# One rounding operation of 2048 columns per unit and engine, with five fixed slots for its parts

## The chip, the cores and the metric

The kernel runs on one core of a Trainium2 chip. Its time is the device time of one execution in microseconds (us), the median over several runs. A core has a matrix engine (PE, whose weight loads are shown as PEld), VectorE (DVE), ScalarE (ACT), GpSimd (POOL) and SyncE (SP, which issues most transfers here). Each engine takes its instructions strictly in order and waits on semaphores for what other engines or transfers deliver.

## The reference, cut to what matters

One decoder layer over 256 tokens of width 2048: latent attention with 16 heads and a short gated convolution side by side, each with a gate, merged by sigmoid gates, then one output projection.

```python
h = _rmsnorm(x, pre_norm_g)
proj = jnp.einsum('bsd,de->bse', h, w_in)          # then cut into ten parts
q = jnp.einsum('bsr,re->bse', _rmsnorm(q_a, q_a_norm_g), w_q_b)
kv = jnp.einsum('bsr,re->bse', _rmsnorm(c_kv, kv_a_norm_g), w_kv_b)
...
attn = attn.reshape(b, s, MLA_WIDTH) * jax.nn.silu(z_mla)
y_mla = jnp.einsum('bse,ed->bsd', attn, w_o_mla)
...
y_conv = jnp.einsum('bse,ed->bsd', b_gate * conv * jax.nn.silu(z_conv), w_o_conv)
merged = jax.nn.sigmoid(g_mla) * y_mla + jax.nn.sigmoid(g_conv) * y_conv
out = jnp.einsum('bsd,de->bse', merged, w_out)
x = x + _rmsnorm(out, post_norm_g)
```

All of it is float32. The kernel makes float32 products on PE out of three products of rounded parts: each operand is split into a high part (the value rounded) and a low part (what the rounding left), and hi x hi, hi x lo and lo x hi are added.

## The kernel before, in words

**Units.** The weights come in units of 128 partitions by 2048 columns (1 MB, `UNIT`, L38), loaded by SP into three rotating buffers `raw`. Before PE can use a unit it is rounded: `split_act` (L264 to L271) writes the high part with one ScalarE operation (L265, `whi`) and the low part with one VectorE subtraction (L266, `wlo`). It does so by halves of 1024 columns (`HALF`), so a unit takes two operations on each engine. The halves lie in two pools of five rotating tiles each, tags `whi` and `wlo`. A half's buffer comes free when PE has done its last product from the half five places earlier.

**PE's work on a unit.** A plain unit is 24 products of 512 columns: first 16 with high weights (against the high and the low part of the activations), then 8 with low weights. Through the first 16 it alternates: four products with the first half, four with the second, and again; then two and two of the 8. A paired unit is 12 products: 8 and 4.

**The stages.** From the start to about 75 us come the latent projections and the gates of the first heads. Then 16 heads follow, each with its own weights (`group_a`, `group_r`, `values`, `channels`) and its softmax, to about 595 us. Behind the heads stands one list, `seq`, of units. It holds plain blocks of four units (their accumulators are named `sq`, the units 115 to 118 being the first block, over the attention output `at_both`), and between them four sets of paired units (`s0` to `s3`, accumulators `sX`, `sY`, `sZ`), which form products of sums of weights: names Q1, V5, V6, V7, V3, V4, Q2, two units each. Where the operand of a paired unit is a sum, VectorE adds two units first (L1272, 2048 columns). V5's operand of the first set is `first_rt` after `first_rb` was added, V6's is the same tile after `first_rc` was added too. Units 113 and 114 are Q1 of the first set and are rounded from `first_rt0` and `first_rt1`. At the end comes the out projection.

**What sets the order.** `ahead` loads up to three units and rounds one unit ahead of the one taken. Behind the heads the loop at L1440 walks over `seq`: for position j it first issues the rounding of the units up to j + 2, then the products of j. Within one engine the order of the program isn't kept as written: a scheduler moves instructions by its own estimate of times, except those marked with `keep_in_program_order` (the last two arguments of `split_act` decide that for a rounding). So a change of what is issued moves instructions on ACT and DVE, and their order is then fixed for every execution.

**The last head.** In the last head (h = 15) `split_branch(3)` rounds the last quarter of the attention output `at_f` into `at_both3`. Ahead of it unit 115 is loaded and rounded (L1101).

Of the kernel before, what the change touches and what calls it, by code (L numbers as in the profile page):

```python
# [12 lines left out]
F32R = mybir.dt.float32r  # L13
# [5 lines left out]
P = 128  # L19
# [63 lines left out]
def tile_layer(ctx: ExitStack, tc: tile.TileContext, xw, w0, xb, x, pos, pvec, post_g, wc, wz, wcv, wkr, wqk, wqr, wv, cwr, wsq, out):  # L83
# [64 lines left out]

    raws, splits, early = {}, {}, {}
# [26 lines left out]
    def split_unit(i):  # L176
        t, w = raws.pop(i), plan[i][1]
        parts = []
        if i == u_kr:
            t = t[:, :w].rearrange("p (k c) -> p k c", k=KD)  # L180
            for h in range(2):
                both = wpool.tile([P, HALF], F32R, name=f"whi{i}_{h}", tag="whi", bufs=5)
                both = both[:, :].rearrange("p (k j c) -> p k j c", k=KD // 2, j=2)
# [5 lines left out]
        if i <= u_qa[-1]:  # L189

            hi, lo = (wpool.tile([P, HALF], F32R, name=f"{o}{i}", tag=o, bufs=5) for o in ("whi", "wlo"))
# [6 lines left out]
            return  # L198
        for h in range(0, w, HALF):
            n = min(HALF, w - h)  # L200
            if u_out[3, 0] <= i < u_out[3, 3]:
                both = spool.tile([P, 2, HALF], F32R, name=f"whl{i}_{h}", tag=LAST[len(last_parts)], bufs=1)
                last_parts.append(both)
                hi, lo = both[:, 0, :], both[:, 1, :]
            else:
                hi = wpool.tile([P, HALF], F32R, name=f"whi{i}_{h}", tag="whi", bufs=5)
                lo = wpool.tile([P, HALF], F32R, name=f"wlo{i}_{h}", tag="wlo", bufs=5)
            split_act(hi[:, :n], lo[:, :n], t[:, h : h + n], i in (u_head[0][1], *u_first, *u_d[0][2][:2]), i in (u_grp["r", 0], u_grp["v", 0], u_head[0][0]))
            parts.append((hi, lo))
# [407 lines left out]
    def group_a(g, together=False):  # L617
# [8 lines left out]
        if g == 0:  # L626

            fs = list(fs)
            ahead(u_grp["v", 0])
# [364 lines left out]
    for h in range(H):  # L994
# [105 lines left out]
        if h == H - 1:  # L1100
            load_raw(done["raw"])  # L1101
            split_unit(done["split"])
            done.update(raw=done["raw"] + 1, split=done["split"] + 1)
# [22 lines left out]
    last_parts = []  # L1126
# [123 lines left out]
    def paired(i, n, c, combine):  # L1250
# [14 lines left out]
        def split(name, u, src, plus, then):  # L1265
            def go():
# [6 lines left out]
                out = []  # L1273
                for h in range(2):
                    hi = wpool.tile([P, HALF], F32R, name=f"shi{i}_{name}{u}_{h}", tag="whi", bufs=5)
                    lo = wpool.tile([P, HALF], F32R, name=f"slo{i}_{name}{u}_{h}", tag="wlo", bufs=5)
                    split_act(hi[:, :], lo[:, :], t[:, h * HALF : (h + 1) * HALF])
                    out.append((hi, lo))
                if then:
                    add_by_transfer(raw[then[0], u], then[1], 2 + u)  # L1280
                return pieces(out)
# [156 lines left out]
    ns = 0  # L1438
    ready = {}
    for j in range(-1, len(seq)):  # L1440
        while loads and loads[0][1] <= j:
            loads.pop(0)[2]()
        if j < 0:
            continue
# [224 lines left out]
```

## Time and profile before

| | us |
|---|---|
| median of 3 runs | 1013.83 (1013.68 to 1014.23) |
| the profiled execution | 1013.55 |
| its span | 1011.8 |
| PE busy | 1004.2 (99%) |
| DVE busy | 811.4 (80%) |
| ACT busy | 586.3 (58%) |
| POOL busy | 170.7 (17%) |

The granted clock of PE was 0.998 of full speed. A profile row of a group reads: line, engine, operation, out<-in with sizes, count, busy time and mean ns of one, then the engine's idle time just before them and what ended it. A row of the timeline begins with the start in us and a duration, and ends with how many instructions in a row it stands for; the last result of the row can lie a little behind the next start, since an engine begins the next operation before the last one's end. In a row of PE's waits stands who waited, for whom, and for how long in total, how often and the longest.

### The profile page before, as it was taken

How to read it: one execution, taken by the hardware profiler on the slowest of the kernel's cores; microseconds unless marked ns; L12 is line 12 of the kernel's file. 1: busy time of each engine (PE TensorE's matmuls, PEld its weight loads, DVE VectorE, ACT ScalarE, POOL GpSimd, SP SyncE). 2: the span in 40 equal slices, each digit the busy share in tenths (PEclk: the TensorE clock that was granted, in tenths of full speed). 3: DMA queues.
4: the chain of work that ended last, by engine and by line, in shares of the span. 5: the costliest groups of instructions: out<-in, count | busy, mean ns of one | idle time of the engine just before them, and what ended most of it. 6: DMA issues, size and time to landing. Idle time of an engine off the chain costs nothing.

```text
span 1011.8 us, 12983 instructions
## 1 busy us (share of the span) xinstructions
PE 1004.2 (99%) x4552; PEld 835.4 (83%) x4552; DVE 811.4 (80%) x1111; ACT 586.3 (58%) x838; POOL 170.7 (17%) x311
## 2 busy tenths in 40 slices
PE   9999999999999999999999999999999999999997
PEld 7888888888888888888888888888888888888886
DVE  7588878868888689877797889898989779997562
ACT  7675656556556456555565465565675664674541
POOL 4620411113211223212133110000000001003000
PEclk9999999999999999999999999999999999999999
DMA  8785768568786668866689779897599989639742
GB/s 338 282 291 183 260 201 304 197 214 276 234 303 232 228 229 283 272 219 232 216 264 338 292 306 291 344 375 218 187 333 296 305 321 260 239 127 322 289 166 84
DMA packets 54369, 261.84 MB, mean 259 GB/s; under 512 B 8768, under 2 KB 13504, under 8 KB 29216
## 3 DMA queue, kind: packets, MB, share of 16 engines
q1 hardware_dynamic: 37728, 214.35, 57.7%
q0 software_dynamic: 12256, 38.13, 14.0%
q10 hardware_dynamic: 4320, 8.54, 2.4%
q8 instruction: 35, 0.57, 0.2%
q14 instruction: 30, 0.25, 0.1%
HBM read 234.80 MB, written 22.02 MB: 254 GB/s over the span
## 4 chain that ended last, share of the span: by engine, by line
PE 98%; DMA 1%; DVE 0%; ACT 0%; SPq 0%; issue 0%
PE cv L88 34%; PE sq L88 17%; PE sX L88 9%; PE z L88 9%; PE out L88 9%; PE sZ L88 4%; PE kn L88 2%; PE qn L88 2%; PE vv L88 2%; PE sY L88 2%; PE ckv L88 2%; PE qa L88 2%; PE qr L88 1%; PE o L88 1%; PE sw L88 1%; DMA raw<-xb_dram 1%
## 5 line engine op out<-in xcount | busy, mean ns | idle before, releaser
L265 ACT ACTIVATE whi<-raw 128x1024 fp32r<-128x1024 f32 (+1 forms) x302 | 306.1, 1028 | 236.7 <-PE cv L88 103.9
L266 DVE TENSOR_TENSOR wlo<-raw,whi 128x1024 fp32r<-128x1024 f32 (+1 forms) x300 | 352.7, 1188 | 101.2 <-ACT whi L265 74.6
L88 PE MATMUL cv<-whi,x_both 128*128 128x512 f32 x1024 | 319.8, 389 | 0.0
L88 PEld LDWEIGHTS cv<-whi,x_both 128*128 128x128 f32 x1024 | 192.3, 188 | 39.5
L88 PE MATMUL cv<-wlo,x_both 128*128 128x512 f32 x512 | 199.5, 390 | 0.0
L88 PEld LDWEIGHTS cv<-wlo,x_both 128*128 128x128 f32 x512 | 96.2, 188 | 19.4
L266 DVE TENSOR_TENSOR slo_V<-b,shi_V 128x1024 fp32r<-128x1024 f32 x60 | 71.5, 1218 | 15.9 <-PE sq L88 8.5
L265 ACT ACTIVATE shi_V<-b 128x1024 fp32r<-128x1024 f32 x60 | 61.5, 1053 | 39.2 <-PE sq L88 21.2
L88 PE MATMUL z<-whi,x_both 128*128 128x512 f32 x256 | 80.0, 389 | 0.0
L366 POOL DMA_DIRECT2D far<-via x64 | 35.4, 559 | 227.2 <-DVE via L358 217.2
L88 PE MATMUL sq<-whi,at_both 128*128 128x512 f32 x256 | 60.6, 389 | 0.0
L88 PE MATMUL sq<-whi,cv_both 128*128 128x512 f32 x256 | 60.6, 389 | 0.0
L88 PEld LDWEIGHTS sq<-whi,cv_both 128*128 128x128 f32 x256 | 48.0, 188 | 10.0
L88 PEld LDWEIGHTS sq<-whi,at_both 128*128 128x128 f32 x256 | 48.0, 188 | 10.0
L88 PEld LDWEIGHTS z<-whi,x_both 128*128 128x128 f32 x256 | 48.1, 188 | 9.9
L88 PE MATMUL z<-wlo,x_both 128*128 128x512 f32 x128 | 49.8, 389 | 0.0
L88 PE MATMUL out<-whi,m_both 128*128 128x512 f32 x208 | 49.4, 389 | 0.0
L88 PE MATMUL sX<-shi_V,form 128*128 128x512 f32 x192 | 47.4, 389 | 0.0
L88 PEld LDWEIGHTS out<-whi,m_both 128*128 128x128 f32 x208 | 39.0, 188 | 8.1
L88 PEld LDWEIGHTS sX<-shi_V,form 128*128 128x128 f32 x192 | 36.0, 188 | 7.5
L265 ACT ACTIVATE shi_Q<-b 128x1024 fp32r<-128x1024 f32 x28 | 28.8, 1052 | 21.5 <-PE sq L88 19.1
L1263 POOL DMA_DIRECT2D b<-wsq_dram x8 | 7.0, 869 | 193.4 <-DVE b L1272 76.8
(304 smaller groups left out, 1568.7 us busy)
## 6 DMA issues: line engine op xcount, KB each, us to landing
raw<-wcv_dram SPq DMA_DIRECT2D x64, 1024.0 KB, 6.2
raw<-wsq_dram SPq DMA_DIRECT2D x48, 1024.0 KB, 7.2
b<-wsq_dram SPq DMA_DIRECT2D x26, 1024.0 KB, 5.7
raw<-wz_dram SPq DMA_DIRECT2D x16, 1024.0 KB, 4.9
raw<-wqk_dram SPq DMA_DIRECT2D x8, 1024.0 KB, 6.8
b<-wsq_dram POOLq DMA_DIRECT2D x8, 1024.0 KB, 11.0
far_form<-form ACTq DMA_DIRECT2D x28, 256.0 KB, 3.3
form<-far_form SPq DMA_DIRECT2D x7, 1024.0 KB, 13.8
```

The costliest lines, as they stand in the source:

```text
L88: return tc.keep_in_program_order(nc.tensor.matmul(*a, **kw))
L265: a = nc.scalar.activation(hi, src, AF.Copy)
L266: b = nc.vector.tensor_tensor(lo, src, hi.bitcast(F32), op=ALU.subtract)
L366: tc.keep_in_program_order(queue.dma_start(out=f[i], in_=m))
L1263: tc.keep_in_program_order(nc.gpsimd.dma_start(out=dst[:, :], in_=wsq[n, c + b, k], accum_op=ALU.add))
```

## The change

Two fixed areas `whi` and `wlo` of five slots each, 1024 columns to a slot, take the place of the two rotating pools. Parts take the next slot in turn, modulo five: a half takes one, a whole unit two; a unit that would take slots 4 and 0 gets them in sorted order, its first half in slot 0.

Behind the heads a unit is rounded by one operation of 2048 columns on ACT and one on DVE. Unit 115 is still rounded by halves, and its second half is issued only at the start of `seq`, behind `split_branch(3)`. In the loop over `seq` the first two units are rounded up front, and from then on the rounding of units up to j + 2 is issued behind the products of j. In the first head's `group_a`, `ahead` is called with `split=0`, so that the unit behind `v0` (unit 20) isn't rounded at that place any more. Three units of the out projection that lay in the spool areas take one area for the high and one for the low part. Heads and everything before them keep rounding by halves, in the new slots.

```diff
@@ -146,6 +146,22 @@
     out_order += [(c, k) for c in (2, 3) for k in range(4)]
     u_out = {ck: add(wsq[4, ck[0], ck[1]]) for ck in out_order}
 
+    PARTS = 5
+    part_area = {o: wpool.tile([P, PARTS, HALF], F32R, name=o) for o in ("whi", "wlo")}
+    part_n = {"whi": 0, "wlo": 0}
+
+    def half_part(o):
+        k = part_n[o] % PARTS
+        part_n[o] += 1
+        return part_area[o][:, k, :]
+
+    def unit_part(o):
+        a, b = sorted((part_n[o] + j) % PARTS for j in range(2))
+        part_n[o] += 2
+        return part_area[o][:, a : b + 1 : b - a, :]
+
+    by_halves = lambda hi, lo: [(hi[:, h, :], lo[:, h, :]) for h in range(2)]
+
     raws, splits, early = {}, {}, {}
     done = {"raw": 0, "split": 0, "end": u_first[1] + 1}
 
@@ -173,14 +189,15 @@
         if i == u_ckv[1]:
             tc.keep_in_program_order(nc.sync.dma_start(out=x_tok, in_=x))
 
-    def split_unit(i):
+    halves = {u_d[0][2][0]: []}
+
+    def split_unit(i, only_first=False):
         t, w = raws.pop(i), plan[i][1]
         parts = []
         if i == u_kr:
             t = t[:, :w].rearrange("p (k c) -> p k c", k=KD)
             for h in range(2):
-                both = wpool.tile([P, HALF], F32R, name=f"whi{i}_{h}", tag="whi", bufs=5)
-                both = both[:, :].rearrange("p (k j c) -> p k j c", k=KD // 2, j=2)
+                both = half_part("whi").rearrange("p (k j c) -> p k j c", k=KD // 2, j=2)
                 ks = slice(h * KD // 2, (h + 1) * KD // 2)
                 split_act(both[:, :, 0], both[:, :, 1], t[:, ks])
                 parts.append(both.rearrange("p k j c -> p k (j c)"))
@@ -188,7 +205,7 @@
             return
         if i <= u_qa[-1]:
 
-            hi, lo = (wpool.tile([P, HALF], F32R, name=f"{o}{i}", tag=o, bufs=5) for o in ("whi", "wlo"))
+            hi, lo = (half_part(o) for o in ("whi", "wlo"))
             for j in range(2):
                 k, o = 2 * i + j, j * XW
                 src = x_first if k == 0 else t[:, o : o + S]
@@ -196,16 +213,30 @@
                 split_act(hi[:, j * R : (j + 1) * R], lo[:, j * R : (j + 1) * R], t[:, o + S : o + XW], True)
             splits[i] = [(hi, lo)]
             return
+        keep, later = i in (u_head[0][1], *u_first, *u_d[0][2][:2]), i in (u_grp["r", 0], u_grp["v", 0], u_head[0][0])
+        if i == u_d[0][2][0]:
+            for h in range(len(halves[i]), 2):
+                if h == 0 or not only_first:
+                    hi, lo = half_part("whi"), half_part("wlo")
+                    split_act(hi, lo, t[:, h * HALF : (h + 1) * HALF], keep)
+                    halves[i].append((hi, lo))
+            splits[i] = halves[i]
+            if only_first:
+                raws[i] = t
+            return
+        if i >= u_first[0]:
+            if u_out[3, 0] <= i < u_out[3, 3]:
+                tags = LAST[2 * (i - u_out[3, 0]) :]
+                hi, lo = (spool.tile([P, 2, HALF], F32R, name=f"w{o}l{i}", tag=tag, bufs=1) for o, tag in zip("hl", tags))
+            else:
+                hi, lo = unit_part("whi"), unit_part("wlo")
+            split_act(hi[:, :, :], lo[:, :, :], t[:, :].rearrange("p (h s) -> p h s", h=2), keep, later)
+            splits[i] = by_halves(hi, lo)
+            return
         for h in range(0, w, HALF):
             n = min(HALF, w - h)
-            if u_out[3, 0] <= i < u_out[3, 3]:
-                both = spool.tile([P, 2, HALF], F32R, name=f"whl{i}_{h}", tag=LAST[len(last_parts)], bufs=1)
-                last_parts.append(both)
-                hi, lo = both[:, 0, :], both[:, 1, :]
-            else:
-                hi = wpool.tile([P, HALF], F32R, name=f"whi{i}_{h}", tag="whi", bufs=5)
-                lo = wpool.tile([P, HALF], F32R, name=f"wlo{i}_{h}", tag="wlo", bufs=5)
-            split_act(hi[:, :n], lo[:, :n], t[:, h : h + n], i in (u_head[0][1], *u_first, *u_d[0][2][:2]), i in (u_grp["r", 0], u_grp["v", 0], u_head[0][0]))
+            hi, lo = half_part("whi"), half_part("wlo")
+            split_act(hi[:, :n], lo[:, :n], t[:, h : h + n], keep, later)
             parts.append((hi, lo))
         splits[i] = parts
 
@@ -626,7 +657,7 @@
         if g == 0:
 
             fs = list(fs)
-            ahead(u_grp["v", 0])
+            ahead(u_grp["v", 0], split=0)
         for j, f in enumerate(fs):
             split_act(qn[0][:, j, :], qn[1][:, j, :], f[:, :])
         for j, f in enumerate((k or keys())()):
@@ -1099,8 +1130,8 @@
             arrive()
         if h == H - 1:
             load_raw(done["raw"])
-            split_unit(done["split"])
-            done.update(raw=done["raw"] + 1, split=done["split"] + 1)
+            split_unit(done["split"], True)
+            done["raw"] += 1
             finish_all(values(h, pt))
             split_branch(3)
         if at == 3:
@@ -1123,7 +1154,6 @@
     wides = right.enter_context(tc.tile_pool(name="wides", bufs=1, side="right", reuse_waits="tile"))
     spool = right.enter_context(tc.tile_pool(name="spool", bufs=1, side="right", reuse_waits="tile"))
     LAST = ("f5", "f6", "rb0", "rc0", "rc1", "rb1")
-    last_parts = []
 
     def form_tile(pool, n):
         return pool.tile([P, KH, 2, P], F32R, name=f"form_{n}", tag=f"f{n}", bufs=1)
@@ -1270,15 +1300,11 @@
                 t = raw[src]
                 if plus:
                     nc.vector.tensor_tensor(t[:, :], t[:, :], raw[plus][:, :], op=ALU.add)
-                out = []
-                for h in range(2):
-                    hi = wpool.tile([P, HALF], F32R, name=f"shi{i}_{name}{u}_{h}", tag="whi", bufs=5)
-                    lo = wpool.tile([P, HALF], F32R, name=f"slo{i}_{name}{u}_{h}", tag="wlo", bufs=5)
-                    split_act(hi[:, :], lo[:, :], t[:, h * HALF : (h + 1) * HALF])
-                    out.append((hi, lo))
+                hi, lo = unit_part("whi"), unit_part("wlo")
+                split_act(hi[:, :, :], lo[:, :, :], t[:, :].rearrange("p (h s) -> p h s", h=2))
                 if then:
                     add_by_transfer(raw[then[0], u], then[1], 2 + u)
-                return pieces(out)
+                return pieces(by_halves(hi, lo))
             return go
 
         def mm(b, f, u, first, last):
@@ -1435,23 +1461,23 @@
         need = pos[id(s0[name][0])]
         loads.append((need - 1, need - AHEAD, lambda n=n: bring_form(n)))
     loads.sort(key=lambda l: (max(l[1], -1), l[0]))
-    ns = 0
-    ready = {}
+    ready = {ns: seq[ns][1]() for ns in range(2)}
+    ns = 2
     for j in range(-1, len(seq)):
         while loads and loads[0][1] <= j:
             loads.pop(0)[2]()
         if j < 0:
             continue
+        w = ready.pop(j)
+        if seq[j][2]:
+            seq[j][2](w)
+        now[0] = j
         while ns < min(j + 3, len(seq)):
             ready[ns] = seq[ns][1]()
             ns += 1
-        now[0] = j
         while j + 3 - (done["split"] - u_out[0, 0]) > len(seq) and done["split"] < u_out[0, 0] + 2:
             split_unit(done["split"])
             done["split"] += 1
-        w = ready.pop(j)
-        if seq[j][2]:
-            seq[j][2](w)
         for fn in pending.pop(j, []):
             fn()
         if seq[j][3]:
```

PE's, POOL's and SP's orders are the same before and after, apart from names. On ACT and DVE three places differ in a way that moves a rounding past other work. In the rows, `whi`/`wlo` with a number and an offset are the halves of that raw unit before; after, `whi_77` and `wlo_78` are the two areas, and the unit is told by its input.

The first place, ACT at the end of the last head: `at_both3` is the last quarter of the attention output, `first_rt1` is unit 114. Before:

```order
L265 ACTIVATE whi114_1024_5710<-first_rt1_5284 128x1024
L265 ACTIVATE at_both2_5714<-at_f_109 128x4x128 x2
L433 ACTIVATE half_5743<-o15_5737 128x256
L811 ACTIVATE cg_5723<-cv15_1_5542,r_both_97 128x512
L265 ACTIVATE whi115_0_5729<-raw115_5727 128x1024
L265 ACTIVATE whi115_1024_5733<-raw115_5727 128x1024
L265 ACTIVATE at_both3_5747<-at_f_109 128x4x128 x2
L265 ACTIVATE whi116_0_5814<-raw116_5789 128x1024
```

The same place of ACT after:

```order
L296 ACTIVATE whi_77<-first_rt1_4896 128x2048
L296 ACTIVATE at_both2_5286<-at_f_111 128x4x128 x2
L464 ACTIVATE half_5309<-o15_5303 128x256
L842 ACTIVATE cg_5295<-cv15_1_5138,r_both_99 128x512
L296 ACTIVATE whi_77<-raw115_5299 128x1024
L296 ACTIVATE at_both3_5313<-at_f_111 128x4x128 x2
L296 ACTIVATE whi_77<-raw115_5299 128x1024
L296 ACTIVATE whi_77<-raw116_5355 128x2048
```

The second half of unit 115 moved from ahead of `at_both3` to behind it. On DVE the low part of `first_rt1` now stands behind the first `cv_w` of the last head, and a transpose stands ahead of the last `at_f`.

The second place, DVE at the end of the first plain block (units 115 to 118) and the first units of V5 (`slo0_V50`, `slo0_V51`; after: the roundings from `first_rt0` and `first_rt1`). Before:

```order
L266 TENSOR_TENSOR wlo117_0_5839<-raw117_5791,whi117_0_5838 128x1024
L266 TENSOR_TENSOR wlo117_1024_5843<-raw117_5791,whi117_1024_5842 128x1024
L1272 TENSOR_TENSOR first_rt0_5283<-first_rt0_5283,first_rb0_5776 128x2048
L1272 TENSOR_TENSOR first_rt1_5284<-first_rt1_5284,first_rb1_5777 128x2048
L266 TENSOR_TENSOR wlo118_0_5875<-raw118_5811,whi118_0_5874 128x1024
L266 TENSOR_TENSOR wlo118_1024_5879<-raw118_5811,whi118_1024_5878 128x1024
L266 TENSOR_TENSOR slo0_V50_0_5911<-first_rt0_5283,shi0_V50_0_5910 128x1024
L266 TENSOR_TENSOR slo0_V50_1_5915<-first_rt0_5283,shi0_V50_1_5914 128x1024
```

The same place of DVE after:

```order
L297 TENSOR_TENSOR wlo_78<-raw117_5357,whi_77 128x2048
L1302 TENSOR_TENSOR first_rt0_4895<-first_rt0_4895,first_rb0_5342 128x2048
L1302 TENSOR_TENSOR first_rt1_4896<-first_rt1_4896,first_rb1_5343 128x2048
L297 TENSOR_TENSOR wlo_78<-first_rt0_4895,whi_77 128x2048
L1302 TENSOR_TENSOR first_rt0_4895<-first_rt0_4895,first_rc0_5346 128x2048
L297 TENSOR_TENSOR wlo_78<-raw118_5379,whi_77 128x2048
```

V5's first unit and the addition of `first_rc0` moved ahead of unit 118. On ACT too the high part of V5's first unit stands ahead of that of 118 now; before it stood behind.

The third place, DVE in the first head: `qn_lo`, `kn` and `qr` are the low parts of queries and keys, `rp_a` and `rp_b` steps of the rotary embedding. Before:

```order
L434 TENSOR_TENSOR f_867<-qn0_1_843,half_868 128x256
L266 TENSOR_TENSOR wlo20_0_874<-raw20_828,whi20_0_873 128x1024
L266 TENSOR_TENSOR wlo20_1024_878<-raw20_828,whi20_1024_877 128x1024
L266 TENSOR_TENSOR qn_lo_853<-f_863,qn_hi_852 128x256
L266 TENSOR_TENSOR qn_lo_853<-f_867,qn_hi_852 128x256
...
L512 TENSOR_TENSOR f_925<-rp_a_929,rp_b_930 128x256
L266 TENSOR_TENSOR qr_920<-f_925,qr_920 64x256 x2
L266 TENSOR_TENSOR vv_lo_942<-vv0_0_943,vv_hi_941 128x512
```

The same place of DVE after:

```order
L465 TENSOR_TENSOR f_809<-qn0_1_785,half_810 128x256
L297 TENSOR_TENSOR qn_lo_795<-f_805,qn_hi_794 128x256
...
L543 TENSOR_TENSOR f_859<-rp_a_863,rp_b_864 128x256
L297 TENSOR_TENSOR qr_854<-f_859,qr_854 64x256 x2
L297 TENSOR_TENSOR wlo_78<-raw20_776,whi_77 128x1024 x2
L297 TENSOR_TENSOR vv_lo_876<-vv0_0_881,vv_hi_875 128x512
```

The two low halves of unit 20 moved from ahead of `qn_lo` to behind `qr`.

## The prediction

> **What bounds the kernel now.** I read the page first, then the waits of PE, then busy time by stage.
>
> ```profile
> span 1011.8 us, 12983 instructions
> PE 1004.2 (99%) x4552; PEld 835.4 (83%) x4552; DVE 811.4 (80%) x1111; ACT 586.3 (58%) x838; POOL 170.7 (17%) x311
> PE 98%; DMA 1%; DVE 0%; ACT 0%; SPq 0%; issue 0%
> PE fin L88 <- ACT dg L1541: 0.9, 1, 0.9
> PE idle L88 <- PEq L1657: 0.8, 1, 0.8
> PE qa L88 <- ACT whi L265: 0.6, 2, 0.3
> ```
>
> PE is busy in 99% of the span, holds 98% of the chain that ended last, and its waits in the whole execution add up to 2.3 us: two at the start, one at the end, none between. So nothing that the change takes off VectorE (DVE) or ScalarE (ACT) comes back as time unless PE's own work gets shorter, and every new wait of PE is paid in full. The question is only whether each rounded unit still arrives before PE needs it.
>
> ```profile
> 640.00:670.00 30.00, 30.00 (x134) 24.82 (x134) 28.69 (x25) 20.47 (x22) 0.00 (x0) 1.00 0.84 333
> 916.00:1003.00 87.00, 87.00 (x386) 72.03 (x385) 47.49 (x54) 35.77 (x47) 7.67 (x14) 1.00 0.59 215
> 595.55 21.76 PE sq L88 x96
> 617.32 5.44 PE sZ L88 x24
> ```
>
> The windows give busy time of PE, PEld, DVE, ACT, POOL. In 640 to 670 DVE has 1.31 us free in 30; in the out projection it is busy 55%. A product costs 226.7 ns in either kind of stretch (21.76/96, 5.44/24). So a plain unit of 24 products is 5.44 us of PE, a paired unit of 12 is 2.72.
>
> **The price of a large operation.** Behind the heads, from about 590 us:
>
> ```profile
> L266 DVE TENSOR_TENSOR wlo<-raw,whi 128x1024 fp32r<-128x1024 f32 x67 | 80.3, 1218 | 6.5 <-ACT whi L265 3.2 <-PE sY L88 1.8 <-PE sX L88 1.4
> L1272 DVE TENSOR_TENSOR b<-b,b 128x2048 f32<-128x2048 f32 x16 | 36.5, 2283 | 0.3 <-DMA b<-wsq_dram 0.3
> L265 ACT ACTIVATE whi<-raw 128x1024 fp32r<-128x1024 f32 x69 | 71.1, 1052 | 34.2 <-PE sX L88 13.2 <-DMA raw<-wsq_dram 8.9 <-PE sY L88 6.8
> L265 ACT ACTIVATE cv_both<-turned_cv 128x512 fp32r<-128x512 f32 x8 | 4.6, 619 | 2.2 <-DMA turned_cv<-far_cv 2.2
> 605.97 4.48 DVE L1272 TENSOR_TENSOR first_rt<-first_rt,first_rb 128x2048 f32<-128x2048 f32 x2
> 610.37 2.35 DVE L266 TENSOR_TENSOR wlo<-raw,whi 128x1024 fp32r<-128x1024 f32 x2
> ```
>
> No rounding of 2048 columns is in the trace. Its nearest row on DVE is the addition of 2048 columns, the same kind of operation on the same size: 2.28 us, and 2.20 from start to start (4.48 for two). Two halves take 2.35. I take 2.28, with 2 x 1.218 = 2.44 as the upper bound. On ACT, 512 more columns cost 1052 - 619 = 433 ns, so 2048 cost 1.052 + 2 x 0.433 = 1.92 (an estimate); above lies 2.10 for two halves one by one. From an end to the start that it releases I take 0.03 to 0.05. So a unit saves about 0.1 us on each engine, worth nothing behind a PE that doesn't wait.
>
> The Trainium skill, Perfetto Trace Analysis, section Optimizing Scalar/DVE Operations, says that larger operations help throughput where the engine is saturated, at about 60 ns of overhead for each on DVE and 93 ns on ScalarE. By that rule DVE would gain over some 88 units (the rows of halves from 590 us on add up to 175) about 5 us; the waits of PE above leave none of it to be had. The same section says that where these engines aren't saturated but cause bubbles elsewhere, smaller operations may end sooner; by that rule the change goes the wrong way, and the places below are where this trace would show it.
>
> **The part that costs nothing everywhere.** With five slots, a unit shares one slot with the unit two before it. Its hi operation waits for product 12 of 24 of that unit (4 of 12 in a paired one), its lo operation for product 22 of 24 (10 of 12). PE then has the unit between still ahead. For plain units lo starts 0.45 before that unit between, is done 1.83 into it, and is wanted 5.44 + 3.63 after its start, so 7 us of cover hide it. Paired units leave 0.45 + 2.72 + 1.81 = 4.98 us for a lo of 2.28, and an addition of 2.20 fits as well (4.48), two don't. Loads, POOL and PE keep their order. The out projection has the slack of its row. What is left are three places at which ACT and DVE stand in another order.
>
> **Place A, the second half of unit 115 (about 596 us).**
>
> ```profile
> 584.75 2.95 ACT L265 ACTIVATE whi<-first_rt 128x1024 fp32r<-128x1024 f32 x3
> 587.72 1.28 ACT L811 ACT_TABLE_LOAD   x1
> 589.01 0.69 ACT L811 ACTIVATE cg<-cv,r_both 128x512 f32<-128x512 f32 x1
> 589.60 1.05 ACT L265 ACTIVATE whi<-first_rt 128x1024 fp32r<-128x1024 f32 x1
> 595.67 1.15 ACT L265 ACTIVATE at_both<-at_f 128x512 fp32r<-128x512 f32 x2
> 596.73 2.00 ACT L265 ACTIVATE whi<-raw 128x1024 fp32r<-128x1024 f32 x2
> 591.83 0.68 DVE L266 TENSOR_TENSOR at_both<-at_f,at_both 128x512 fp32r<-128x512 f32 x1
> 592.43 0.68 DVE L813 TENSOR_TENSOR cv_w<-cv_w,cg 128x512 f32<-128x512 f32 x1
> 595.23 0.41 DVE L745 TENSOR_TENSOR at_f<-f,at_f 128x256 f32<-128x256 f32 x1
> 595.56 0.70 DVE L358 STREAM_TRANSPOSE mv<-cv_f 128x512 f32<-128x512 f32 x1
> 595.39 3.79 PE L88 MATMUL sq<-whi,at_both 128*128 128x512 f32 x16
> ```
>
> Before, both halves' hi stand ahead of the two at_both3 on ACT. Now the second half stands behind them, and at_both3 waits for at_f on DVE (595.23 + 0.41, then 595.67). PE begins unit 115 at 595.39 and wants the second half with its fifth product, 595.39 + 4 x 0.2267 = 596.30. The walk: hi of first_rt0 from 584.75 takes 1.92, to 586.67; the table load and cg follow at the old spacing (1.28, 0.59), so hi of first_rt1 starts at 588.54 and ends 590.45. Its lo on DVE runs from 590.48, and 2.20 later at_both2 starts, 592.68 instead of 591.83. From there to at_f it was 3.40; the one cv_w goes ahead now (-0.60) and the transpose comes between (+0.63): at_f runs 596.11 to 596.52. ACT: the two at_both3 start at 596.55 and take 1.06 to the next start, the second half runs 597.61 to 598.66, and PE goes on at 598.70. **2.4 us.** With at_f as early as before it is 1.5; with the upper prices of the three large operations 2.9.
>
> **Place B, the end of the first plain block (about 612 us).**
>
> ```profile
> 606.27 3.79 PE L88 MATMUL sq<-whi,at_both 128*128 128x512 f32 x16
> 611.71 3.79 PE L88 MATMUL sq<-whi,at_both 128*128 128x512 f32 x16
> 615.34 1.98 PE L88 MATMUL sq<-wlo,at_both 128*128 128x512 f32 x8
> 608.37 2.01 ACT L265 ACTIVATE shi_V<-first_rt 128x1024 fp32r<-128x1024 f32 x2 [0.91 <-DVE first_rt L1272]
> ```
>
> Unit 117 starts at 606.27, 118 at 611.71, and 118's lo is wanted at 615.34, 3.63 later. Before, 118 was rounded ahead of V5's first unit on both engines (610.37 is its lo). Now V5's hi and lo and the addition of first_rc0 stand ahead of 118's, in fixed order, though PE needs 118 first. Let s be the start of unit 117. V5 shares a slot with 117's first half. Hi: V5's waits for 117's twelfth product, s + 2.72; two operations of 1.92 (1.87 to the next start) end at s + 2.77 + 3.79 = s + 6.6, where PE wants 118 at s + 5.44: 1.15. Lo: the slot is free with product 22, s + 4.99; V5's lo from s + 5.02, the addition from s + 7.22, 118's lo from s + 9.42 to s + 11.70, wanted at s + 9.07. What PE lost for hi lies inside this: **2.65 us** in all. Bounds: 2.55 if the last one too takes its spacing of 2.20; 3.3 with 2.44 for each rounding and the slot freed at the modelled end of the product (0.16 later). Before, no wait stood here, because nothing of V5 stood ahead of 118. After it V5 is long ready, so the loss isn't passed on.
>
> **Place C, the first head's queue on DVE (about 87 us).**
>
> ```profile
> 80.79 0.42 ACT L265 ACTIVATE qn_hi<-f 128x256 fp32r<-128x256 f32 x1 [0.25 <-DVE f L434]
> 81.01 2.34 DVE L266 TENSOR_TENSOR wlo<-raw,whi 128x1024 fp32r<-128x1024 f32 x2
> 83.27 0.75 DVE L266 TENSOR_TENSOR qn_lo<-f,qn_hi 128x256 fp32r<-128x256 f32 x2
> 89.13 0.87 DVE L266 TENSOR_TENSOR qr<-f,qr 64x256 fp32r<-64x256 f32 x2 [0.48 <-ACT qr L265]
> 87.34 0.39 PE L88 MATMUL cv<-wlo,x_both 128*128 128x512 f32 x1
> ```
>
> The two lo halves of unit 20 were rounded at 81.01, ahead of qn_lo; with split=0 they stand behind qr. The chain from qn_lo to qr can start at 80.79 + 0.42 = 81.21, 2.06 earlier than 83.27. So qr ends at 89.13 + 0.87 - 2.06 = 87.94, and the first half of unit 20 at 87.94 + 1.18 = 89.1. PE wants it at 87.34: 1.8. If the chain gains the whole 2.34 that was taken out, it is 1.45; if a hop to ACT eats the gain, up to 3.8. I take **1.65**, since only one row of it (qr, 0.48) waits for ACT.
>
> **Sum.** 1013.55 (the profiled execution, span 1011.8 and 1.75 around it) + 2.4 + 2.65 + 1.65 = 1020.25. The median lies 0.28 above that execution: 1020.5.
>
> **Rivals.** *DVE becomes the bound in the paired runs.*
>
> ```profile
> 644.35 3.79 PE L88 MATMUL sq<-whi,at_both 128*128 128x512 f32 x16
> 646.31 2.29 DVE L1272 TENSOR_TENSOR first_rt<-first_rt,b 128x2048 f32<-128x2048 f32 x1 [0.32 <-DMA b<-wsq_dram]
> ```
>
> Behind the plain unit that starts at p = 644.35 come V3, V4, Q2, six paired units with two additions. If the first operand lands as late as here, p + 1.96, then addition, sc, V3 twice, addition, V4 follow as 2.20 + 0.60 + 3 x 2.20 + 2.28 to p + 13.64, where V4 is wanted at p + 5.44 + 5.44 + 1.81 = p + 12.69: 0.95 lost. If it has landed (A and B give the loads 5 us more), V4 ends at p + 11.70 and 1.0 is left. Three more sets have about 0.6 to 2 us of slack; with 2.44 a rounding two of them would lose as much: 1021.5 to 1023.5. *The places stall less*, since the chains A and C have hops that I know only from one execution: 1014 to 1017. *Nothing stalls*, because hi and lo come early enough after all: 1013.8; B speaks against it, as its three DVE operations would have to take 1.34 each. *Faster*: PE waits on fewer semaphores, two for a unit instead of four. If each wait removed gave back time, the three stalls would have to be paid first: 6.7 us over some 88 units and two waits each is 38 ns a wait. A plain unit has one wait in six products, a paired one in three, and both run at 226.7 ns a product, so I price a wait at nothing; the point from which this decides is 38 + 2.03/176 = 50 ns a wait: under 1011.8.
>
> **How the numbers follow.** Forecast (all three, no more) 0.62, the paired runs too 0.18, smaller stalls 0.11, nothing 0.05, faster 0.04. The forecast's own bounds are 1.5 + 2.55 + 1.45 = 5.5 and 2.9 + 3.3 + 3.8 = 10.0, unlikely all at once; 1018.5 to 1022.5 is its own range. The range asked for, 1016.8 to 1023.5, takes in most of the two rivals beside it. A difference under 0.2%, 2 us, can't be told from no change here: faster 0.04, same 0.07 (nothing, and the least of the smaller stalls), slower 0.89.
>
> **What would show it.** Right: PE's waits name at_both-unit 115 on ACT (about 2.4), unit 118 on ACT and DVE (1.15 and 1.5), and cv behind unit 20's lo on DVE (1.65); DVE's rounding of 2048 columns reads 2.28, ACT's 1.92; a product stays at 226.7. Wrong: no wait of PE beyond 2.3 us, or products that run faster than 226.7 ns, or waits spread over the paired runs.

## The result, and the profile after

The changed kernel takes 1023.66 us (median of 6 runs, 1021.34 to 1028.4), the kernel before 1013.6 us in the same comparison. The ratio is 1.0104, with a 95% interval of 1.008 to 1.0129: slower, as forecast, but by 10 us instead of 6.7, and 0.16 us above the range. The times scatter far more than before (7 us against 0.9). The profiled execution of it took 1026.13 us, 2.5 above the median.

From the page of the changed kernel:

```profile
span 1024.4 us, 12582 instructions
...
PE 1007.8 (98%) x4552; PEld 836.1 (82%) x4552; DVE 805.6 (79%) x1008; ACT 576.4 (56%) x735; POOL 170.7 (17%) x311
```

Its table of PE's waits (engine and line, for whom; us in total, how often, the longest):

```profile
PE sq L88 <- ACT whi L296: 5.0, 3, 2.2
PE cv L88 <- DVE wlo L297: 2.9, 1, 2.9
PE sq L88 <- DVE wlo L297: 1.4, 1, 1.4
```

DVE and ACT do less (811.4 to 805.6, 586.3 to 576.4), and it buys nothing. PE, which waited for nothing in the middle of the program, waits 9.3 us for roundings now. The same PE instructions run in the same order in both kernels, so their start times can be laid side by side; wherever the difference grows, time is lost there. The rows of the changed kernel at those places, PE first (the idle time and its releaser stand in brackets), then the rows of DVE and ACT that PE waited for:

```profile
89.77 0.50 PE L88 MATMUL cv<-wlo,x_both 128*128 128x512 f32 x1 [2.89 <-DVE wlo L297]
...
602.88 3.02 PE L88 MATMUL sq<-whi,at_both 128*128 128x512 f32 x12 [2.25 <-ACT whi L296]
...
619.73 3.96 PE L88 MATMUL sq<-whi,at_both 128*128 128x512 f32 x16 [1.14 <-ACT whi L296]
625.12 2.12 PE L88 MATMUL sq<-wlo,at_both 128*128 128x512 f32 x8 [1.43 <-DVE wlo L297]
...
770.38 3.96 PE L88 MATMUL sq<-whi,cv_both 128*128 128x512 f32 x16 [1.65 <-ACT whi L296]
...
600.73 1.15 ACT L296 ACTIVATE at_both<-at_f 128x512 fp32r<-128x512 f32 x2 [3.24 <-DVE at_f L776]
...
618.25 2.29 DVE L297 TENSOR_TENSOR wlo<-first_rt,whi 128x2048 fp32r<-128x2048 f32 x1 [3.04 <-PE sq L88]
...
767.37 1.16 ACT L296 ACTIVATE cv_both<-turned_cv 128x512 fp32r<-128x512 f32 x2 [4.79 <-DMA turned_cv<-far_cv]
```

The first four PE rows are the three forecast places: unit 20, unit 115, and unit 118 for its hi and its lo. The fifth was not forecast: unit 131, the first of the convolution branch, whose hi on ACT stands behind two roundings (cv_both, 767.37) that wait for a transfer. SP had issued that transfer only when a lo operation on DVE had freed its buffer, by the table of waits of SP between 740 and 770 us:

```profile
SPq L989 <- DVE wlo L297: 1.3, 1, 1.3
```

The operations themselves have the forecast prices, in the listing by shape between 600 and 929 us:

```profile
L297 DVE TENSOR_TENSOR wlo<-raw,whi 128x2048 fp32r<-128x2048 f32 x32 | 73.2, 2287 | 12.0 <-ACT whi L296 11.9
...
L296 ACT ACTIVATE whi<-raw 128x2048 fp32r<-128x2048 f32 x33 | 63.3, 1918 | 36.1 <-PE sX L88 15.3 <-PE sZ L88 6.8 <-PE sY L88 6.5
```

One more loss has no row among the waits. Windows of the changed kernel; the column behind POOL is PE's granted clock:

```profile
88.00:92.00 4.00, 2.23 (x6) 1.79 (x7) 3.94 (x7) 3.55 (x4) 0.00 (x0) 0.78 0.07 4
92.00:96.00 4.00, 4.00 (x15) 3.20 (x15) 3.46 (x4) 0.44 (x1) 0.00 (x0) 0.79 0.35 96
```

From 92 to 96 us PE is busy all the time and yet begins 15 products instead of the 17 to 18 that 226.7 ns give. The clock record shows half clock from 90.23 us for 3.41 us, right behind the wait at unit 20. Products start every 0.43 us in it, and 1.73 us are lost.

A second profile of the same kernel (the first experiment below) shows what stands in both executions. Each cell is the growth of the difference to the kernel before, from the start times of the products, in us; what PE needs to be back at full pace behind a wait is counted with the half clock where both come together:

| place | forecast | first profile | second profile |
|---|---|---|---|
| unit 115 (A) | 2.4 | 2.55 | 2.39, and 1.64 at half clock |
| unit 118 (B) | 2.65 | 3.20 | 3.20 |
| unit 20 (C) | 1.65 | 3.05, and 1.73 at half clock | 2.39, and 1.76 at half clock |
| unit 131 | 0 | 2.00 | 0.20 |
| all else (0.6 and 0.8 earlier at the start, small ones later) | 0 | 0.05 | -0.52 |
| span against the kernel before | 6.7 | 12.6 | 11.1 |

### The profile page after: what moved, and what is told of

The parts are those of the page before. It is cut to its first block, busy times and chain, and to the rows that moved or that the text cites. A ratio compares the mean times of both kernels' runs of the same rounds, so it can differ in the third digit from the quotient of the medians.

```text
span 1024.4 us, 12582 instructions
## 1 busy us (share of the span) xinstructions
PE 1007.8 (98%) x4552; PEld 836.1 (82%) x4552; DVE 805.6 (79%) x1008; ACT 576.4 (56%) x735; POOL 170.7 (17%) x311
## 5 line engine op out<-in xcount | busy, mean ns | idle before, releaser
L296 ACT ACTIVATE whi<-raw 128x1024 fp32r<-128x1024 f32 (+2 forms) x258 | 300.4, 1173 | 242.1 <-PE cv L88 109.2
L297 DVE TENSOR_TENSOR wlo<-raw,whi 128x1024 fp32r<-128x1024 f32 (+2 forms) x256 | 348.4, 1368 | 108.9 <-ACT whi L296 95.8
L296 ACT ACTIVATE whi<-b 128x2048 fp32r<-128x2048 f32 x44 | 84.5, 1920 | 61.9 <-PE sq L88 37.4
L297 DVE TENSOR_TENSOR wlo<-b,whi 128x2048 fp32r<-128x2048 f32 x44 | 100.3, 2288 | 20.1 <-ACT whi L296 12.5
L88 PE MATMUL sX<-whi,form 128*128 128x512 f32 x256 | 63.3, 389 | 0.0
L88 PEld LDWEIGHTS sX<-whi,form 128*128 128x128 f32 x256 | 48.0, 188 | 10.0
L1302 DVE TENSOR_TENSOR b<-b,b 128x2048 f32<-128x2048 f32 x16 | 36.6, 2285 | 2.6 <-DMA b<-wsq_dram 2.5
```

The lines of the kernel that those rows point to most:

```text
L88: return tc.keep_in_program_order(nc.tensor.matmul(*a, **kw))
L296: a = nc.scalar.activation(hi, src, AF.Copy)
L297: b = nc.vector.tensor_tensor(lo, src, hi.bitcast(F32), op=ALU.subtract)
L1302: nc.vector.tensor_tensor(t[:, :], t[:, :], raw[plus][:, :], op=ALU.add)
```

## The experiments

Two theories stood against each other. **Order**: with five slots and the new places of issue, ACT and DVE stand in another order at a few places, and each place costs its own wait. **Size**: operations of 2048 columns are too coarse wherever DVE is nearly full, whatever the order.

### The changed kernel a second time

No edit.

> The changed kernel itself, profiled a second time. It tells the waits that stand in every execution from those that come and go: its six times lie between 1021.3 and 1028.4. Theory 1 (three places set by order): the waits at units 20, 115 and 118 come back within 0.3 us of 3.05, 2.4 and 3.1; the half clock behind unit 20 and the wait at unit 131 may be longer, shorter or absent, and make up the spread. Theory 2: other places, or these by more than 1 us otherwise.

Measured: 1023.82 us (1022.82 to 1024.62), before on the same chip 1012.97. The waits at the three places came back (the last column of the table): B within 0.1, A within 0.2, C 0.7 shorter, 0.4 beyond what was expected of it. The wait at unit 131 was all but absent (0.20). The half clock appeared twice here, behind unit 20 and behind unit 115. Windows of this run:

```profile
598.00:602.00 4.00, 1.85 (x9) 1.19 (x7) 4.00 (x7) 2.07 (x4) 0.00 (x0) 0.98 0.73 297
602.00:606.00 4.00, 3.92 (x11) 3.12 (x12) 4.00 (x6) 2.55 (x4) 0.51 (x1) 0.59 0.19 29
```

In the first profile a wait of the same length at unit 115 left the clock at 1.00:

```profile
600.00:604.00 4.00, 1.75 (x8) 1.13 (x7) 4.00 (x7) 3.27 (x4) 0.00 (x0) 1.00 0.43 178
```

So the three places came back where they had been, and half clock and unit 131 come and go: with 1.6 to 2 us apiece they are large enough for the scatter of the times, though the other executions have no trace to show it in.

### Unit 118 ahead of V5

```diff
-        keep, later = i in (u_head[0][1], *u_first, *u_d[0][2][:2]), ...
+        keep, later = i in (u_head[0][1], *u_first, *u_d[0][2]), ...
...
-                split_act(hi[:, :, :], lo[:, :, :], t[:, :].rearrange("p (h s) -> p h s", h=2))
+                split_act(hi[:, :, :], lo[:, :, :], t[:, :].rearrange("p (h s) -> p h s", h=2), i == 0 and name == "V5")
```

> The changed kernel with the roundings of unit 118 kept ahead of V5's first unit on ACT and DVE, nothing else; every value is computed as in the changed kernel. Theory 1: PE's waits at unit 118 (1.1 for hi, 1.4 for lo in the profile, 3.1 with the restarts of PE) fall to nothing, the time by 3 us to 1019 to 1021.5. Theory 2 (DVE is short of time there whatever its order): at least 1.5 us of it comes back at V5's units or at the additions.

Measured: 1022.05 us (1019.93 to 1023.70) beside 1023.82 for the changed kernel on the same chip. PE's waits of this run:

```profile
PE cv L88 <- DVE wlo L297: 2.5, 1, 2.5
PE sq L88 <- ACT whi L296: 2.2, 1, 2.2
PE sZ L88 <- DVE wlo L297: 0.9, 1, 0.9
```

Both waits at unit 118 are gone, and nothing came back at V5 or at the additions of the first set: there the order was the whole cause. The third row is at 895 us, in the last paired set, where the changed kernel lost 0.3 in its profile; so a part of the gain was lost again further on (1.2 by the starts of the products). This profile also has the half clock behind both unit 20 and unit 115. The median fell by 1.8, not by 3; its range overlaps that of the changed kernel, so the trace carries this reading, not the time.

### Unit 20 and unit 115 early: what the slots don't allow

The first tries to mend the other two places simply took back their edits. The first took back the one at unit 20.

```diff
-            ahead(u_grp["v", 0], split=0)
+            ahead(u_grp["v", 0])
```

> The changed kernel with one thing undone: in the first head unit 20 is rounded ahead of qn_lo again. Theory 1 (order: each place at which ACT or DVE stands in another order costs its own wait, and the wait at unit 20 also costs the half clock that follows it): the wait of cv on wlo (2.9 us) and the 3.4 us at half clock are gone, 4.8 us less than in the profiled execution of the changed kernel, so 1018 to 1021; the waits at units 115 (2.2) and 118 (1.1 + 1.4) stay as they are. Theory 2 (the engines are slower as a whole with large operations, and a place that is mended shows up elsewhere): no more than 2 us better, with new waits of PE in the heads.

The next one also rounds both halves of unit 115 in the last head and keeps unit 118 ahead of V5.

```diff
-                if h == 0 or not only_first:
+                if h == 0 or h == 1:
```

> The changed kernel with the order before at all three forecast places: unit 20 early, both halves of unit 115 ahead of at_both3, unit 118 ahead of V5's first unit. All units behind the heads still go by one operation of 2048 columns. Theory 1: only the wait at the first unit of the convolution branch is left, 1.65 to 1.9 us in the changed kernel: 1014.5 to 1016. Theory 2: above 1018, the waits move to the paired runs, where DVE has 1 to 2 us free in 30.

The third adds a fixed order for cv_both2 and cv_both3, behind units 131 and 132.

```diff
-        keep, later = i in (u_head[0][1], *u_first, *u_d[0][2]), ...
+        keep, later = i in (u_head[0][1], *u_first, u_d[0][3][0], *u_d[0][2]), ...
...
-            def go(keep=False):
+            def go(keep=both.name == 'cv' and first == 2):
```

> As the kernel with the three places mended, and the roundings of cv_both2 and cv_both3 kept behind units 131 and 132, so that ACT doesn't wait for their transfer ahead of unit 131. Theory 1: no wait of PE above 0.3 us is left between 10 us and the out projection's end, 1013.2 to 1014.2, no different from the kernel before. Theory 2: above 1016. A third reading, that fewer and larger operations gain once nothing waits: below 1012.

The fourth rounds by halves again on top of that.

```diff
-                split_act(hi[:, :, :], lo[:, :, :], ...)
+                for h in range(2):
+                    split_act(hi[:, h, :], lo[:, h, :], t[:, h * HALF : (h + 1) * HALF], ...)
```

> As the kernel with four places mended, but each unit behind the heads goes by two operations of 1024 columns again, in the same slots and with the same issue behind the older products. Theory 1 (order decides, the size of an operation doesn't): within 1 us of the kernel with four places mended and of the kernel before, 1013 to 1014.5. Theory 2 (size costs): faster than the one with four places mended by more than 2 us.

Measured: 1030.16, 1031.22, 1036.45 and 1031.71 us, against 1013.08 before. All four changed what is computed: the keys' products of the first head read unit 20's parts, and in the last three Q1's products read parts of unit 115. A rotating buffer can be asked for early and waits until it is free; the kernel before makes the same early call, and PE has no wait at the keys' products (`kn`). A slot of a fixed tile is simply written at its place in the program, and a reader that comes later in the program reads the new data. PE's products then wait for the unit that overwrote their slot, as in the first of the four:

```profile
PE kn L88 <- DVE wlo L297: 4.7, 1, 4.7
...
PE kn L88 <- ACT whi L296: 2.1, 1, 2.1
```

So these runs say nothing for or against either theory on places A and C. They show what the late issue is for: with five slots it isn't a choice. The order of the third also made a new wait of 2.5 us for the lo of the third unit of the convolution branch, whose rounding stood behind an addition that waited for its transfer. That mending is a miss.

### Three places mended within the five slots

Unit 118 as above; unit 20 rounded as soon as the keys' products are issued, ahead of the rotary chain; the last quarter of the attention output rounded behind unit 115's second half.

```diff
-            ahead(u_grp["v", 0], split=0)
...
         for j, f in enumerate((k or keys())()):
             split_act(kn[:, 0, j, :], kn[:, 1, j, :], f[:, :])
+        if g == 0: ahead(u_grp["v", 0])
...
             finish_all(values(h, pt))
-            split_branch(3)
...
             ns += 1
+        if j == 0: split_branch(3)
```

> The changed kernel, every value as in it, with three places mended within the five slots: unit 118 ahead of V5's first unit; the last quarter of the attention output rounded behind the second half of unit 115; unit 20 rounded once the keys' products are issued, ahead of the rotary chain instead of behind it. Theory 1: only the wait at unit 131 (0 to 2 us) and up to 0.5 us at unit 21 are left, no half clock: 1013.5 to 1016.5. Theory 2 (large operations cost by themselves): above 1018, with waits of PE in the paired runs.

> As the kernel with three places mended, but with two operations of 1024 columns for each unit on each engine, in the same slots and issued at the same places of the program. Theory 1 (the order decides, not the size): within 2 us of the kernel with three places mended, 1013.5 to 1016. Theory 2 (size): 3 us or more faster than it. Where the scheduler's order differs, its waits will show it.

Measured on one chip in one comparison: **1016.37 us** with large operations (ratio 1.0036, 1.0023 to 1.0048) and **1013.86** with halves (1.0009, 1.0000 to 1.0018), before 1012.97. PE's waits, first with large operations (the two rows left out, fin and idle, are the ones that the kernel before has as well):

```profile
PE sZ L88 <- DVE wlo L297: 1.4, 1, 1.4
PE sq L88 <- ACT whi L296: 1.0, 1, 1.0
...
PE qa L88 <- ACT whi L296: 0.4, 1, 0.4
PE sq L88 <- DVE wlo L297: 0.3, 1, 0.3
```

and with halves:

```profile
PE qa L88 <- ACT whi L297: 0.5, 1, 0.5
PE cv L88 <- DVE wlo L298: 0.3, 1, 0.3
```

The three places are gone in both, and neither kernel's profile has a stretch of half clock before the end of the products. The 7.4 us between the changed kernel and this one are the order and what it draws behind it. But the size isn't free either: 2.5 us are left that halves don't have, between what the two theories allowed (2 at most, 3 at least). The sZ row is V3's second unit in the first paired set. DVE in the kernel with large operations, then in the one with halves:

```profile
646.09 2.29 DVE L1303 TENSOR_TENSOR first_rt<-first_rt,b 128x2048 f32<-128x2048 f32 x1 [1.19 <-DMA b<-wsq_dram]
...
648.89 2.28 DVE L297 TENSOR_TENSOR wlo<-first_rc,whi 128x2048 fp32r<-128x2048 f32 x1
651.10 2.28 DVE L1303 TENSOR_TENSOR first_rt<-first_rt,b 128x2048 f32<-128x2048 f32 x1
653.30 2.28 DVE L297 TENSOR_TENSOR wlo<-first_rc,whi 128x2048 fp32r<-128x2048 f32 x1
```

```profile
644.83 1.23 DVE L298 TENSOR_TENSOR wlo<-first_rc,whi 128x1024 fp32r<-128x1024 f32 x1 [0.37 <-PE sX L88]
...
646.66 2.29 DVE L1304 TENSOR_TENSOR first_rt<-first_rt,b 128x2048 f32<-128x2048 f32 x1
648.87 2.35 DVE L298 TENSOR_TENSOR wlo<-first_rc,whi 128x1024 fp32r<-128x1024 f32 x2
```

With halves, V3's first unit slips in ahead of the addition that waits for its transfer, and the second follows the first addition at once. With large operations both units stand behind an addition each, and the second is ready at 655.6. The sq row of 1.0 is unit 131 again; with halves its first half stands ahead of the late transfer on ACT.

### The changed kernel by halves

All moves of the change, but two operations for a unit (the edit of the fourth kernel above, alone).

> The changed kernel with its slots, its issue behind the older products and all its moves, but each unit behind the heads by two operations of 1024 columns on each engine. Theory 1 (the five slots and the order that comes with them cost, the size of an operation adds a part): the waits at units 20 (2.4 to 3.1) and 115 (2.4) stay, the one at 118 falls from 3.1 to 1.5 to 2, as the first half of its lo is ready 1.1 earlier, and nothing at unit 131 or in the paired runs: 1019.5 to 1023. Theory 2 (the large operations cost): below 1017.

Measured: 1020.35 us (ratio 1.0068, 1.0053 to 1.0083), before 1013.25. The size of the operation gives back 3 to 4 us of the 10; 7 belong to the slots and the order that comes with them. Each beside the kernel before on its own chip, the four kernels stand at 10.9 us (changed, large), 7.1 (changed, halves), 3.4 (three places mended, large) and 0.9 (mended, halves). Halves also let the scheduler choose another order, so the effect of size holds that of the order which a large operation shuts out. Large operations in rotating buffers were not run; what the five slots cost apart from the late issue that they force stays open. From its table of PE's waits, unit 20:

```profile
PE cv L88 <- DVE wlo L298: 2.3, 1, 2.3
```

and from its timeline, unit 115:

```profile
601.07 3.01 PE L88 MATMUL sq<-whi,at_both 128*128 128x512 f32 x12 [1.36 <-ACT whi L297]
```

Unit 115 waits 1.36 instead of 2.25, which had been expected to stay: with halves on first_rt0 and first_rt1 the chain ahead of at_f ends earlier (at_f starts 0.16 ahead of unit 115's first product; in the changed kernel, 0.75 behind it). Unit 118 fell further than expected, to 0.3 for hi and 0.4 for lo, unit 131 didn't wait, and the half clock came once, behind unit 20.

### Two tries at the rest

Into the kernel with three places mended: the transfer for the convolution branch one place earlier, and V3 kept ahead of V4's additions.

```diff
-        "Q1": cv_u[:1] + v[0][:1] + cv_u[1:2] + v[0][1:2], "V5": cv_u[2:3] + v[0][2:3] + cv_u[3:], ...
+        "Q1": cv_u[:1] + v[0][:1] + cv_u[1:3] + v[0][1:2], "V5": v[0][2:3] + cv_u[3:], ...
```

> As the kernel with three places mended, with the third of the four rounding steps of the convolution branch one place earlier in the list, so that its transfer (turned_cv) stands ahead of two weight loads on SP instead of behind them, and its rounding ahead of Q1's second unit on ACT. Theory 1 (unit 131 waits only because ACT stands at a late transfer): the wait of 1.0 to 1.2 us at unit 131 is gone, 1014.5 to 1016 with the wait at V3's second unit (1.4) left. Theory 2 (the transfers are short of bandwidth there): a wait of a like size comes up at another unit between 740 and 800.

```diff
-                    nc.vector.tensor_tensor(t[:, :], t[:, :], raw[plus][:, :], op=ALU.add)
+                    added = nc.vector.tensor_tensor(t[:, :], t[:, :], raw[plus][:, :], op=ALU.add)
+                    if i == 0 and name == "V4": tc.keep_in_program_order(added)
...
-                split_act(..., i == 0 and name == "V5")
+                split_act(..., i == 0 and name in ("V5", "V3", "V4"))
```

> As the kernel with three places mended, with V3's two units of the first set rounded on DVE ahead of the additions for V4, which wait for a transfer. The scheduler then places Q2's first unit ahead of V4's second. Theory 1 (order on DVE again): the wait at V3's second unit (1.4 and its restart) is gone; Q2 ahead of V4's second unit costs 0 to 2 us, since it waits for products of V4's first: 1014 to 1017. Theory 2 (DVE has not enough time in this run with large operations): a wait of 1.5 us or more at V4 or Q2 that no order explains.

Measured: 1016.79 us (1.0035, 1.0023 to 1.0047) and 1021.34 us (1.0078, 1.0061 to 1.0095), before 1013.25. In the first the wait at unit 131 is gone, and 0.3 (0.6 by the starts of the products) came up at the paired unit ahead of it, for its lo; the median is above what was expected and no better than without the move, so this one settles nothing about bandwidth. In the second the wait at V3's second unit is gone, but V4's first unit waits 0.8 us for its hi, and its second 2.9. ACT shows why the second does:

```profile
658.85 1.92 ACT L296 ACTIVATE whi<-b 128x2048 fp32r<-128x2048 f32 x1 [1.74 <-DVE wlo L297]
661.00 1.91 ACT L296 ACTIVATE whi<-first_rt 128x2048 fp32r<-128x2048 f32 x1 [0.24 <-DVE first_rt L1303]
```

Q2's first unit (from b) stands ahead of V4's second (from first_rt), and that waits for an addition which DVE now does last. PE stood for 3.1 us and lost 2.6 more at half clock behind it. The forecast of 0 to 2 us for that order was a miss. No version found here beats the kernel before.

## Why the prediction was right or wrong

**What bounds the kernel: right.** Only PE's waits, and the half clock that they drew behind them, counted; fewer and larger operations on DVE and ACT gave nothing back. A product at full clock stayed at 226.7 ns with half as many waits, which rules out the rival that was faster.

**The prices: right.** 2.287 us on DVE against 2.28, 1.918 on ACT against 1.92. The Trainium skill's rule that was weighed (Perfetto Trace Analysis, Optimizing Scalar/DVE Operations: smaller operations end sooner where these engines cause bubbles elsewhere) agrees with the runs: halves were 2.5 us faster with three places mended.

**The sum: the step that failed.** It took three waits, each at its own length, and put all else at nothing. The first profile lost 5.9 us more than the 6.7 of the sum: 2.0 at unit 131, 1.7 at half clock, 1.4 at place C, 0.55 at B, 0.15 at A. The second lost 4.4 more: 3.4 at half clock, 0.7 at C, 0.55 at B, 0.2 at unit 131, less 0.5 elsewhere. The half clock and unit 131, neither of them a term nor a rival, are thus 3.7 and 3.6 us of the miss. The median execution (1023.66) is faster than both of these (1026.13 and 1024.62), and how its own miss divides has no trace.

**The half clock.** Behind a wait it cost 1.6 to 1.8 us each time that it came in these two profiles.

**Unit 131.** "What is left are three places" was wrong. In the kernel before, one half of unit 131 stood on ACT ahead of the late transfer and one behind:

```profile
751.66 1.04 ACT L265 ACTIVATE whi<-raw 128x1024 fp32r<-128x1024 f32 x1
752.96 1.16 ACT L265 ACTIVATE cv_both<-turned_cv 128x512 fp32r<-128x512 f32 x2 [0.25 <-DMA turned_cv<-far_cv]
754.32 1.06 ACT L265 ACTIVATE whi<-raw 128x1024 fp32r<-128x1024 f32 x1 [0.21 <-PE sX L88]
```

A whole unit can stand only on one side, and the scheduler put it behind; in the changed kernel it follows the row at 767.37 above:

```profile
768.43 1.90 ACT L296 ACTIVATE whi<-raw 128x2048 fp32r<-128x2048 f32 x1
```

**Place A: right.** 2.4 against 2.55 and 2.39 by the starts of the products (2.25 in the row of the wait, which counts from the modelled end of the product before); the kernel with it mended lost 0.4 there.

**Place B: right in its mechanism, 0.5 too small.** V5's operations started later into unit 117 than taken, 2.97 us instead of 2.77 for the hi and 5.26 instead of 5.02 for the lo: the slots came free about at the modelled ends of products 12 and 22. For the lo this was one of the two terms of the upper bound. So the wait for hi was 1.3 by the starts of the products (1.14 in its row) against 1.15. PE also took about 0.13 us more after each wait before it was back at full pace, which no term held. Keeping the order of two units removed all of it.

**Place C: right in its place, 0.7 to 1.4 too small.** The chain from qn_lo to qr was to begin at 81.21 and gain 2.06. In the first profile it began at 81.58, and PE was 0.62 earlier, so it gained about 1.1. The step took only rows of DVE and one wait of qr for ACT. What held the chain was ACT ahead of it, in the changed kernel:

```profile
78.68 1.06 ACT L296 ACTIVATE whi<-raw 128x1024 fp32r<-128x1024 f32 x1 [2.79 <-DMA raw<-wcv_dram]
79.65 0.64 ACT L464 ACTIVATE half<-qn 128x256 f32<-128x256 f32 x2
80.18 1.06 ACT L296 ACTIVATE whi<-raw 128x1024 fp32r<-128x1024 f32 x1
81.13 0.41 ACT L296 ACTIVATE qn_hi<-f 128x256 fp32r<-128x256 f32 x1
```

Unit 20's hi waits for its transfer, and the queries' halves stand behind it on ACT. In the second profile the transfer came in time:

```profile
76.82 1.06 ACT L296 ACTIVATE whi<-raw 128x1024 fp32r<-128x1024 f32 x1 [0.15 <-DMA raw<-wcv_dram]
...
80.79 0.42 DVE L297 TENSOR_TENSOR qn_lo<-f,qn_hi 128x256 fp32r<-128x256 f32 x1 [0.15 <-ACT qn_hi L296]
```

There the chain, with PE 0.76 earlier, gained about 1.7, and PE lost 2.39 instead of 3.05. So the late transfer is the difference between the two. The rest of the miss is small pieces: a start 0.3 later than taken, a chain 0.1 longer, and 0.15 between the 1.8 that the prediction's own rows gave and the 1.65 that it took. Both values lie within its bounds of 1.45 to 3.8. "Only one row of it (qr, 0.48) waits for ACT" missed a wait of 0.15 of kn in the kernel before, and it held only as long as DVE's two large rows stood ahead of the chain and gave ACT time.

**The rival on the paired runs** named the right stretch and the right trigger (an operand that lands late, at 646.31 then and 646.09 in the mended kernel) and the right escape: in the changed kernel the waits ahead gave the loads time, and nothing was lost there. Once they were mended, 1.4 us were lost, at V3's second unit and not at V4.

## What to carry to other kernels

Where one engine never waits, count for each change in the order of the engines that feed it what now stands ahead of the work it wants next, on every engine of the chain, including those that had cover before. A fixed slot ties the place of issue to the last reader, so an early load that a rotating buffer allowed becomes a late one. And one operation for a whole buffer can stand only on one side of a late arrival, where two halves can stand on both.

## What the runs showed of the hardware

The half clock follows a rule that the traces of all the kernels here share. The stretches of half clock ahead of the last product begin on a grid of 3.41 us that runs through each trace (one lasts 3.41, 6.83 or 10.24), and each begins at the end of a grid window in which PE stood idle for most of it. Idle time in a window, added up from the start times of the products against 226.7 ns, for every full-clock window behind 84 us and up to the last product with more than 1.4 us of it, in the 13 profiles:

| idle in a window of 3.41 us | windows | followed by half clock |
|---|---|---|
| 1.43 to 1.84 us | 10 | 0 |
| 2.12 to 3.41 us | 11 | 11 |

Ahead of 84 us products of other sizes make the count rougher; the windows there fit it too, the closest with about 2.0 us of idle, one of them followed by half clock and one not.

So a wait of 2.4 us costs nothing more when the grid cuts it in two, as at unit 115 in the first profile (1.76 in the fuller window), and about 1.6 us more when one window holds most of it, as in the second (2.18). Why the other executions scatter as they do has no trace of its own: that it is this and unit 131 is worked out from two profiles. By the table the threshold lies between 1.84 and 2.12 us, 54 to 62% of a window. The Trainium skill (TensorE: Matmul & The Clock Gate, Part 1: The HAM clock gate) gives a free-running window of 3413 ns, which the traces show too, and has PE fall back to half clock after at least one idle window. Here the measurement differs: a window with 2.12 us of idle was enough.
